# A mixer's order list: the triangular inverse's first step moved up, and five of the delta rule's steps placed between S5's output quarters

## The chip, the cores and the metric

The kernel runs on one core of one Trainium2 chip. A time is the device time of one execution in microseconds (us). The core has five engines that run at once, each with a queue of its own: TensorE (PE in the profile; its weight loads are PEld), VectorE (DVE), ScalarE (ACT), GpSimd (POOL) and SyncE (SP, which issues the transfers here). They wait for each other by semaphores.

## The reference, cut to what matters

```python
for l in range(DEPTH):                       # 2 layers, 272 tokens (16 meta + 256), 1024 features
    h = h + 0.5 * swiglu(rmsnorm(h, ffn1_norm[l]), ...)     # 2816 wide
    h = h + hybrid_mixer(rmsnorm(h, mix_norm[l]), ...)
    h = h + 0.5 * swiglu(rmsnorm(h, ffn2_norm[l]), ...)

def hybrid_mixer(h, w_in, ..., w_out):
    proj = h @ w_in                          # 1024 x 2312
    sb_q, sb_k, sb_v, dn_qkv, dn_z, dn_b, dn_a, s5_u = split(proj)
    o_sb = rmsnorm(stick_breaking_attention(sb_q, sb_k, sb_v))      # 4 heads of 64
    o_dn = gated_deltanet(dn_qkv, dn_z, dn_b, dn_a, ...)            # 4 heads of 64
    o_s5 = rmsnorm(s5_mixer(s5_u, ...))                             # 512 wide, GELU, then a GLU
    return concatenate([o_sb, o_dn, o_s5]) @ w_out

def gated_deltanet(...):
    q, k, v = split(silu(causal_conv4(dn_qkv)))     # q, k L2-normalised per head
    # chunked: T = inverse(I + strict_lower((beta k) k^T * decay)) per chunk,
    # attn = lower(q k^T * decay), then a recursion over the chunks:
    #   v_new = T (beta v - ... k S),  o = q S + attn v_new,  S = S * e^g + k^T v_new
    return rmsnorm(o) * silu(z)
```

## The kernel before

Features lie on the 128 partitions and tokens along the free axis, so the residual stream is eight blocks of 128 x 272 (`xT`). Each product of a weight with the stream is made of three matmuls in a reduced fp32 form: both operands are split into a high and a low part (`wh`, `wl`, `xh`, `xl`; `mm3`, lines 141 to 143). `weights` loads a block of 512 KB, ScalarE copies out the high part (line 133), and VectorE, or for a few blocks by number GpSimd, subtracts for the low part (line 136). The products inside the groups are plain fp32 matmuls.

The change is in `mixer`, which each layer runs once between its two feed-forward parts. Its steps are functions or generators, and the string `MIX` is the order in which they are traced: a letter names a step, a digit its block; a letter without a digit advances a generator to its next `yield`. The program order that follows is a priority: a planner then fixes each engine's queue at compile time, earlier steps first, and puts a later step's instruction ahead where it counts on an earlier one not being ready. On the chip each queue runs in the fixed order. The letters that matter:

- `C0` to `C5`: projections and convolutions of the delta rule's q (0, 1), k (2, 3) and v (4, 5). `U`, `Q`, `K`, `V`, `Z`: projections of S5's input, of the attention's q, k, v, and of the gate z. Each is one block of weights and 24 matmuls (`unit`).
- `g` (`dn_gates`, 7 steps): gates, k's norm, the decay matrix `E`; the last one makes `LT`, k's products times the decay (`dn_products`, line 883).
- `i` (`dn_inverse`, 9 steps): the inverse of the unit lower triangular matrices. The first step gathers the diagonal blocks (`L32`, `LT8`, `r8` on VectorE), spreads them by one matmul (line 995), and solves the 8 x 8 blocks on GpSimd with a row of 14 dependent small operations (lines 1009 and 1010). The others double the block size by small matmuls; the last one (line 1078) completes `TTf`.
- `r` (`dn_rest`, 11 steps): r1 the norms of q (`pn`, line 1099), r2 q's products (`dn_products`, into `E`), r3 the transposes of v and k (line 1114), r4 `pvn`, the first product with `TTf` (line 1153), r5 the first state (`pS`, lines 1159 and 1161), r6 `pk` with that state (line 1143), r7 and r8 the second chunk's `pvn` and `pS`, r9 to r11 the last 16 tokens (`pkt`, `pvt`). r1 to r3 need only the convolutions after their SiLU, not the inverse.
- `l`: SiLU of q and v, then ScalarE's table for GELU. `p`, `t`, `y`: S5's inputs, states and outputs of one quarter (`pY`, lines 845 and 847, with GELU). `x`: the GLU in two halves (`pglu`).
- `a` (`sb`, 10 steps): the attention; the last two (`pob`, line 1275) are its outputs. `v` transposes its values.
- `n`: ScalarE's table for Ln and Exp. `m`: the norm factor `R5` of S5's part. `S4`, `S6`, `S0`, `S2`: the rows of `w_out` that S5's part feeds; their evictions (`sy`, line 1424) need `R5`. `o`: the delta rule's norm and output (`po`). Behind the list come the other rows of `w_out`, four blocks, and the next part's norm.

PSUM has four tags of two buffers each. The tag a step uses:

```python
def s5_outputs(self, u, r):     p = self.psum("b", "pY")
def dn_rest(self, qkv):         psum = lambda nm: self.psum("d", nm)     # r4 to r11
    pn = self.psum("b", "pn")                                            # r1
    self.dn_products(qn, AT, ATt, "b")                                   # r2, three tiles
    pv = self.psum("b", "pv")                                            # r3, three tiles
```

In SBUF the scratch tag `cv` has three buffers, which r1, `Z`, the GLU, the attention's outputs and `sy` share.

Of the kernel before, what the change touches and what calls it, by code (L numbers as in the profile page):

```python
# [38 lines left out]

MIX = "C2 C3 U0 g U1 g g U2 g g g U3 g Q0 p0 p1 Q1 t0 p2 p3 K0 i t1 K1 a a t2 C0 a a i C1 i t3 a a i C4 i a a i C5 l i " \
      "y0 V0 i y1 V1 i y2 Z0 y3 Z1 v r r r r x r r x r n a r r r r a m S4 S6 o S0 S2"
ON_POOL = (5, 7, 10, 15, 20, 25)
NBUF = (3, 2, 3)
LO_POOL = 5
# [14 lines left out]
class Trunk:  # L61
# [1283 lines left out]
    def mixer(self, l, nxt):  # L1345
# [7 lines left out]
        with ExitStack() as es:  # L1353
# [54 lines left out]
            def w_out_part(x, d0, tag):  # L1408
# [11 lines left out]
                for j in range(2):  # L1420
                    x_, p = self.xT[:, d0 + j, t0:], ps[j][:, :T - t0]
                    if x == "S":
# [11 lines left out]
                         m=lambda: self.rms(self.acc, 4 * 512, 0, self.R5, "b"))  # L1434
            for x in MIX.split():
                if x in chains:
# [53 lines left out]
```

## Time and profile before

| | us |
|---|---|
| median of 3 runs (lowest to highest) | 1174.08 (1170.92 to 1177.52) |
| the profiled execution | 1172.99 |
| its span, first to last instruction | 1170.9 |
| TensorE busy in it | 1140.0 (97%) |
| VectorE busy | 858.5 (73%) |
| ScalarE busy | 620.5 (53%) |
| GpSimd busy | 194.0 (17%) |
| mean granted TensorE clock | 0.983 |

Layer 0's mixer lies at about 228 to 390 us of the span, layer 1's at about 808 to 972 us. A window's row gives, for a stretch of the span, each engine's busy time with its number of instructions, the clock granted to TensorE as a share of 2.4 GHz, and the share and rate of the transfers. A timeline's row gives the start, the time, the engine, the line, the operation with the names of its output and inputs, its shape and the number of instructions that were merged; in brackets the engine's idle time just before it and what ended it.

### The profile page before, as it was taken

What the parts mean: (1) busy time and instruction counts of PE and PEld (TensorE: products, weight loads), DVE (VectorE), ACT (ScalarE), POOL (GpSimd) and SP (SyncE); (2) the same over time, 40 slices, a digit from 0 to 9 for tenths busy, and PEclk for the clock granted to TensorE, in tenths of its full rate; (3) what the DMA queues carried; (4) which work ended last, traced back from release to release, by engine and by line L of the source; (5) the groups of instructions that cost most, each with busy time, mean ns of one, the idle gap of its engine ahead of it and who ended that gap; (6) DMA issues with size and microseconds to landing.
All of it is one profiled execution on the core that took longest, in us unless ns stands there. A gap on an engine that the chain in (4) does not pass through costs nothing.

```text
span 1170.9 us, 23748 instructions
## 1 busy us (share of the span) xinstructions
PE 1140.0 (97%) x9544; PEld 1091.7 (93%) x9544; DVE 858.5 (73%) x1609; ACT 620.5 (53%) x993; POOL 194.0 (17%) x242
## 2 busy tenths in 40 slices
PE   8999999999998999999999999999999989999997
PEld 7999999998896999999999999999988969999985
DVE  7999986599656965565569998756995678666544
ACT  6455465464663654444454555645545737545533
POOL 6312101113310111110202111011141001111100
PEclk9999999999998999999999999999999979999998
DMA  5655544542221455555565565455332216556663
GB/s 186 183 174 174 169 149 151 166 127 60 87 73 55 146 172 173 176 180 163 184 180 168 167 193 163 137 179 156 107 91 74 85 43 198 181 181 189 191 196 109
DMA packets 196858, 173.74 MB, mean 148 GB/s; under 512 B 21300, under 2 KB 193004, under 8 KB 196748
## 3 DMA queue, kind: packets, MB, share of 16 engines
q1 hardware_dynamic: 196732, 172.22, 48.6%
q8 instruction: 75, 1.23, 0.4%
q14 instruction: 35, 0.29, 0.1%
q10 hardware_dynamic: 16, 0.00, 0.0%
HBM read 171.15 MB, written 1.05 MB: 147 GB/s over the span
## 4 chain that ended last, share of the span: by engine, by line
PE 83%; DVE 10%; POOL 2%; ACT 2%; issue 2%; DMA 1%; SPq 0%; ACTq 0%; DVEq 0%; POOLq 0%
PE proj L143 17%; PE proj L142 17%; PE proj L141 17%; PE pd L143 5%; PE pd L142 5%; PE pd L141 5%; PE pd L490 5%; DVE wl L136 2%; PE pY L847 1%; POOL TT L1010 1%; PE pm L780 1%; POOL t L1009 1%; PE pob L1275 1%; PE pY L845 1%; DVE s5z L836 1%
## 5 line engine op out<-in xcount | busy, mean ns | idle before, releaser
L141 PE MATMUL proj<-xh,wh 128*128 128x272 f32 (+1 forms) x1840 | 524.8, 291 | 1.5 <-DVE sy L1424 1.5
L142 PE MATMUL proj<-xl,wh 128*128 128x272 f32 (+1 forms) x1840 | 521.9, 290 | 0.3 <-DVE xl L1222 0.3
L143 PE MATMUL proj<-xh,wl 128*128 128x272 f32 (+1 forms) x1840 | 493.4, 291 | 1.5 <-DVE wl L136 1.2
L133 ACT ACTIVATE wh<-raw 128x1024 fp32r<-128x1024 f32 (+1 forms) x324 | 338.2, 1044 | 291.5 <-PE proj L142 102.2
L136 DVE TENSOR_TENSOR wl<-raw,wh 128x1024 fp32r<-128x1024 f32 (+1 forms) x312 | 378.7, 1214 | 146.2 <-PE pd L143 60.5
L141 PEld LDWEIGHTS proj<-xh,wh 128*128 128x128 f32 x1840 | 348.8, 190 | 4.3 <-DVE sy L1424 2.6
L142 PEld LDWEIGHTS proj<-xl,wh 128*128 128x128 f32 x1840 | 348.3, 189 | 2.4 <-DVE xl L1222 0.5
L143 PEld LDWEIGHTS proj<-xh,wl 128*128 128x128 f32 x1840 | 331.4, 189 | 3.9 <-DVE wl L136 2.9
L432 POOL TENSOR_TENSOR hl<-h,hh 128x272 fp32r<-128x272 f32 (+1 forms) x88 | 80.8, 921 | 452.4 <-ACT hh L431 451.5
L141 PE MATMUL pd<-hh,wh 128*128 128x272 f32 x528 | 149.8, 289 | 0.0
L142 PE MATMUL pd<-hl,wh 128*128 128x272 f32 x528 | 149.5, 288 | 0.0
L143 PE MATMUL pd<-hh,wl 128*128 128x272 f32 x528 | 141.1, 289 | 0.2
L141 PEld LDWEIGHTS pd<-hh,wh 128*128 128x128 f32 x528 | 99.3, 188 | 0.2
L142 PEld LDWEIGHTS pd<-hl,wh 128*128 128x128 f32 x528 | 99.4, 188 | 0.1
L143 PEld LDWEIGHTS pd<-hh,wl 128*128 128x128 f32 x528 | 95.2, 189 | 1.0 <-DVE wl L136 0.9
L104 ACT ACTIVATE g<-g 128x272 f32<-128x272 f32 (+2 forms) x92 | 37.7, 415 | 68.8 <-DVE g L426 68.7
L431 ACT ACTIVATE hh<-h 128x272 fp32r<-128x272 f32 (+1 forms) x88 | 36.3, 419 | 50.7 <-DVE h L430 50.6
L430 DVE TENSOR_TENSOR h<-proj,g 128x272 f32<-128x272 f32 (+1 forms) x88 | 37.8, 434 | 32.3 <-PE proj L143 20.6
L426 DVE TENSOR_TENSOR g<-proj,R 128x272 f32<-128x272 f32 (+1 forms) x88 | 37.5, 431 | 18.3 <-PE proj L143 18.1
L428 DVE TENSOR_TENSOR g<-g,R 128x272 f32<-128x272 f32 (+1 forms) x88 | 37.8, 434 | 12.5 <-ACT g L104 12.2
L136 POOL TENSOR_TENSOR wl<-raw,wh 128x1024 fp32r<-128x1024 f32 x12 | 29.4, 2452 | 97.0 <-PE proj L143 31.9
L373 POOL TENSOR_TENSOR acc<-acc,sq 128x272 f32<-128x272 f32 (+1 forms) x20 | 23.1, 1153 | 91.9 <-ACT sq L367 91.3
(490 smaller groups left out, 1295.4 us busy)
## 6 DMA issues: line engine op xcount, KB each, us to landing
raw<-in_ffn_w_gate_dram SPq DMA_DIRECT2D x88, 512.0 KB, 3.6
raw<-in_ffn_w_up_dram SPq DMA_DIRECT2D x88, 512.0 KB, 3.7
raw<-in_ffn_w_down_dram SPq DMA_DIRECT2D x70, 512.0 KB, 3.5
raw<-in_w_in_dram SPq DMA_DIRECT2D x36, 512.0 KB, 4.3
raw<-in_ffn_w_down_dram SPq DMA_DIRECT2D x24, 384.0 KB, 3.0
raw<-in_w_out_dram SPq DMA_DIRECT2D x16, 512.0 KB, 3.4
raw<-in_s_w_glu_dram SPq DMA_DIRECT2D x4, 512.0 KB, 4.7
xin<-in_x_dram SPq DMA_DIRECT2D x4, 256.0 KB, 6.1
```

The lines of the kernel that those rows point to most:

```text
L104: i = self.nc.scalar.activation(out, in_, func, **k)
L133: nc.scalar.activation(h[:, :n], r[:, :n], AF.Copy)
L136: e.tensor_tensor(l[:, :n], r[:, :n], f32(h[:, :n]), op=ALU.subtract)
L141: mm(p, wh, xh, start=first, stop=False)
L142: mm(p, wh, xl, start=False, stop=False)
L143: mm(p, wl, xh, start=False, stop=last)
L426: V.tensor_tensor(g1, pg[j][:, :N], R, op=ALU.mult)
L428: V.tensor_tensor(g1, g1, R, op=ALU.mult)
L430: V.tensor_tensor(h, pu[j][:, :N], g1, op=ALU.mult)
L431: nc.scalar.activation(hh[:, f, :N], h, AF.Copy)
L432: G.tensor_tensor(hl[:, f, :N], h, f32(hh[:, f, :N]), op=ALU.subtract)
L490: PE.matmul(pd[i][e], x[:, f, ts], w[:, 0, e * 512:e * 512 + 512], start=f == 0 and w is h and x is hh, stop=f == NF - 1 and w is lo)
```

## The change

Only the string `MIX` is changed. The inverse's first step `i`, which stood behind `K0`, stands behind the seventh `g`, ahead of `Q0`; the second to the seventh inverse step move up by about one place each, to `K0`, `K1`, `C0`, `C1`, `C4` and ahead of `C5`; the last two stay behind `V0` and `V1`. The first five steps `r`, of which four stood behind `Z1 v` and one behind the GLU's first half, stand behind `l`, `V0`, `y2`, `y3` and `Z1`. The GLU's `x` steps keep their order; r6 stays behind the first, and r7 and r8 stand behind the second, ahead of `n` and the attention's first output.

```diff
--- before.py
+++ after.py
@@ -39,8 +39,8 @@
 
 
 
-MIX = "C2 C3 U0 g U1 g g U2 g g g U3 g Q0 p0 p1 Q1 t0 p2 p3 K0 i t1 K1 a a t2 C0 a a i C1 i t3 a a i C4 i a a i C5 l i " \
-      "y0 V0 i y1 V1 i y2 Z0 y3 Z1 v r r r r x r r x r n a r r r r a m S4 S6 o S0 S2"
+MIX = "C2 C3 U0 g U1 g g U2 g g g U3 g i Q0 p0 p1 Q1 t0 p2 p3 K0 i t1 K1 i a a t2 C0 a i a C1 i t3 a a C4 i a a i C5 l " \
+      "r y0 V0 r i y1 V1 i y2 r Z0 y3 r Z1 r v x r x r r n a r r r a m S4 S6 o S0 S2"
 ON_POOL = (5, 7, 10, 15, 20, 25)
 NBUF = (3, 2, 3)
 LO_POOL = 5
```

## Rows read from the trace of the kernel before

**Rows 1.** Part 1 of the page: busy us, share, instructions.
```profile
PE 1140.0 (97%) x9544; PEld 1091.7 (93%) x9544; DVE 858.5 (73%) x1609; ACT 620.5 (53%) x993; POOL 194.0 (17%) x242
```

**Rows 2.** Windows, layer 0: us, busy us (instructions) per engine, PEclk, DMA.
```profile
224.00:228.00 4.00, 4.00 (x34) 4.00 (x33) 3.53 (x6) 3.06 (x6) 0.50 (x6) 1.00 0.89 247
...
296.00:300.00 4.00, 3.49 (x28) 3.03 (x26) 2.39 (x6) 3.05 (x6) 3.38 (x9) 1.00 0.50 135
300.00:304.00 4.00, 2.13 (x79) 1.68 (x80) 4.00 (x9) 0.81 (x2) 0.11 (x1) 1.00 0.00 0
...
360.00:364.00 4.00, 4.00 (x35) 3.04 (x33) 1.23 (x1) 1.67 (x3) 0.00 (x0) 1.00 0.15 49
364.00:368.00 4.00, 2.02 (x30) 1.49 (x29) 2.52 (x9) 0.98 (x3) 0.00 (x0) 1.00 0.24 82
368.00:372.00 4.00, 3.36 (x24) 1.84 (x25) 2.63 (x7) 1.22 (x3) 0.00 (x0) 0.63 0.01 4
372.00:376.00 4.00, 2.95 (x10) 1.52 (x8) 1.35 (x5) 1.63 (x5) 0.29 (x1) 0.50 0.00 0
376.00:380.00 4.00, 3.57 (x19) 3.25 (x18) 3.96 (x13) 0.95 (x2) 0.00 (x0) 0.59 0.00 0
```

**Rows 3.** The same windows in layer 1's mixer.
```profile
876.00:880.00 4.00, 3.49 (x64) 3.18 (x65) 2.38 (x6) 2.83 (x5) 2.67 (x8) 1.00 0.44 125
880.00:884.00 4.00, 2.58 (x69) 2.13 (x56) 4.00 (x9) 1.34 (x3) 0.11 (x1) 1.00 0.01 4
...
944.00:948.00 4.00, 1.73 (x34) 0.76 (x32) 3.48 (x11) 1.13 (x3) 0.00 (x0) 0.74 0.00 0
948.00:952.00 4.00, 3.93 (x16) 2.06 (x12) 1.67 (x5) 1.02 (x2) 0.00 (x0) 0.50 0.00 0
952.00:956.00 4.00, 2.54 (x8) 1.40 (x8) 2.48 (x8) 1.63 (x5) 0.29 (x1) 0.50 0.00 0
956.00:960.00 4.00, 4.00 (x22) 4.00 (x22) 3.91 (x13) 0.95 (x2) 0.00 (x0) 0.56 0.00 0
```

**Rows 4.** TensorE's timeline at the mixer's end: start, us, line, [idle, releaser].
```profile
361.44 0.67 PE L1275 MATMUL pob<-W 128*64 128x272 f32 x2
...
366.84 0.32 PE L1176 MATMUL pkt<-qkv,kn 64*32 64x64 f32 x7 [1.28 <-DVE qkv L1170]
...
369.26 1.17 PE L1275 MATMUL pob<-W 128*64 128x272 f32 x2 [0.32 <-DVE sby L1284]
...
376.76 0.60 PE L141 MATMUL proj<-xh,wh 128*128 128x272 f32 x1 [0.43 <-DVE sy L1424]
```

**Rows 5.** TensorE's timeline: inverse's end, recursion's steps, the GLU's last product.
```profile
331.55 1.14 PE L1078 MATMUL py<-TTf,X 64*64 64x64 f32 x16
...
340.99 0.50 PE L1099 MATMUL pn<-bd,sq 128*128 128x2 f32 x4
...
347.83 0.29 PE L143 MATMUL pglu<-xh,wl 128*128 128x272 f32 x1
...
351.64 1.11 PE L1153 MATMUL pvn<-vb,TTf 128*128 128x64 f32 x8
...
357.36 0.43 PE L1143 MATMUL pk<-qkv,kn 64*128 64x64 f32 x2
...
363.94 1.10 PE L1161 MATMUL pS<-qkv,E 128*128 128x64 f32 x8
```

**Rows 6.** ScalarE's timeline: the silu step.
```profile
311.26 1.21 ACT L104 ACTIVATE qkv<-qkv 128x544 f32<-128x544 f32 x2
```

**Rows 7.** GpSimd's timeline: the inverse's first step.
```profile
278.95 2.10 POOL L1004 TENSOR_TENSOR Lm<-L,lev 128x288 f32<-128x288 f32 x2 [0.88 <-DVE L L986]
...
299.10 0.80 POOL L1012 TENSOR_TENSOR TT<-TT,m8c 128x288 f32<-128x288 f32 x1
```

**Rows 8.** VectorE: durations of one line (ns, min/median/max); an eviction of r2.
```profile
L825 DVE TENSOR_TENSOR x<-s5z,sn x8: 433/436/1029, 258.2 to 870.6; 128x272 f32<-128x272 f32 x8
...
343.86 0.68 DVE L883 TENSOR_TENSOR E<-pl,E 128x512 f32<-128x512 f32 x1
```

## The prediction

> **What bounds the kernel now.** I read the page's first part, then windows of 4 us through both mixers, then TensorE's timeline in the windows that stood out, and last VectorE's, ScalarE's and GpSimd's timelines for what TensorE waited for there. The page: TensorE is busy for 97% of the span [rows 1]. That leaves 31 us without a matmul, and a busy microsecond need not be a full one. A window of plain projections holds 34 matmuls in 4 us, 0.12 us apart, at a granted clock of 1.00, the 2.4 GHz level; this is the measure [rows 2].
>
> Against it, two places in each mixer fall short. At the end of layer 0's mixer, 364 to 380 us, TensorE is busy 2.02, 3.36, 2.95 and 3.57 us, at clocks of 1.00, 0.63, 0.50 and 0.59 [rows 2]. It loses 4.1 us idle, and of the busy time another 3.36 x 0.37 + 2.95 x 0.50 + 3.57 x 0.41 = 4.2 us to the clock: 8.3 us. The same place of layer 1's, 944 to 960 us, loses 3.8 us idle and 1.73 x 0.26 + 3.93 x 0.50 + 2.54 x 0.50 + 4.00 x 0.44 = 5.4 us to the clock: 9.2 us [rows 3]. Together **17.5 us**; it is an upper bound, since busy times of overlapping matmuls count some of the clock's loss double. The second place, where the attention's scores and the inverse's first matmuls meet, costs 0.51 + 1.87 and 0.51 + 1.42 us idle: **4.3 us** [rows 2, 3].
>
> What is waited for in the tail: the timeline has the delta rule's tokens of the last 16 (`pkt`, 1.28 us idle behind VectorE), then the attention's second output (`pob`), then `w_out`'s products behind `sy` [rows 4]. All of this is chain work with nothing left to lay beside it: the projections are over and the S half of `w_out` has been spent as filler, and what of it remains waits for a PSUM buffer. The slow clock comes with it: the same `pob` product takes 0.67 us for two at the full clock and 1.17 us in the tail [rows 4].
>
> Why the chain is late: the inverse's last product is at 331.55 us, but the recursion's first that uses it, `pvn`, is at 351.64 us [rows 5]. In between stand steps `r`1 to `r`3, which need neither: their first product `pn` is issued at 340.99 us [rows 5], though its operand is ready behind `silu`, which is done at 311.26 + 1.21 = 312.5 us [rows 6]. The list puts them behind `Z1 v`, and the order of the queues keeps to the list while TensorE has earlier work. So a move in the list is a move in the queue.
>
> **The change part by part.** No instruction, transfer or weight block is added or taken away, and the order of the weight blocks among themselves is the same, so SP's queue and the blocks split on GpSimd stay. Everything is order, and the sum is made of idle time and clock, not of durations.
>
> *Steps r1 to r5 go between l and x.* r1 goes right behind `silu`, r2 behind V0, r3 behind y2, r4 behind y3, r5 behind Z1; r6 stays behind the GLU's first half and r7 behind its second; r8 comes in front of the attention's first output instead of behind it. Their own TensorE time is the same on either side. Cover where they go now: V0, V1, Z0 and Z1 are 96 products, 96 x 0.12 = 11.6 us. What it does to the tail, counted from the GLU's last product (347.83 us, call it G) [rows 5]: before, `pvn` (r4) is at G + 3.8, `pk` (r6) at G + 9.5, the last `pS` (r8) ends at G + 17.2. After it, r6 can start 24 products or 2.9 us before G or a little later; r6 to the end of r8 takes 365.0 - 357.4 = 7.7 us in the trace, so r8 ends between G + 4.8 and G + 7.7, and G itself moves back by the products of r4 to r6 put ahead of it, some 4 us by their rows. The chain is then 365.0 - 347.8 - 7.7 - 4 = 5.5 to 8.4 us ahead of where it is now.
>
> Is there enough to lay beside it? Behind G stand the S half of `w_out`, 96 x 0.12 = 11.6 us, two outputs of the attention of 2.1 us each at full clock (two heads; the row gives 0.67 us for a head's first pair), and some 5 us of small products: 21 us. The chain behind r8 is r9 to r11 (365.0 to 369.3 us, 4.2 us) and the delta rule's norm and output, 7.5 us up to the next product of `w_out` (376.76 us); beside it run the two attention outputs, one behind the other, of some 7.5 us each (the first's product at 361.44, the second's at 369.26 us, less its wait of 0.32) [rows 4]. The longer of the two, 15 us, ends at G + 20 to G + 23. So filler and chain are about as long: the tail's loss goes nearly wholly, or 2 us a mixer stay. Bounds: all 17.5 us back, or only what the earlier chain gives in idle time with the clock's part kept, 4 us a mixer, 8 us. I take **13.5 us**, near the upper bound since the window ahead of 364 us is still full at a clock of 1.00 [rows 2], with the chain and the filler side by side, and that is the state the change extends.
>
> *The inverse's first step goes from behind K0 to right behind `g`'s last (k's products).* Its chain is: `LT`, small copies and sums on VectorE, one product, and on GpSimd `Lm` at 278.95 us and a row of small operations up to 299.10 + 0.80 us [rows 7]. Ahead of it on VectorE stood two S5 quarters' states and K's evictions; with these behind it, the chain starts up to 8 us earlier. Queued behind its product on TensorE are Q0 and the quarters' inputs: the product waits in a queue that runs in order, and they with it. In the trace, TensorE's wait for the chain's end (the first product of the next step) and for the scores is the 4.3 us of the second place. Below: these 4.3 us go, since the chain is done before the scores need TensorE. Above: the same wait comes again in front of Q0, 4.3 us more. The nearest rows are the waits themselves, which come from order against real durations and will fall somewhere else rather than go; I take **0.5 us** back.
>
> *The inverse steps i2 to i7* shift by one place (K0, K1, C0, C1, C4, C5); they stand in the same stretch of full TensorE windows, at nothing, hidden by the conv blocks' 24 products each; uncovered they would cost 1 us a step.
>
> Sum: the profiled execution took 1173.0 us, its span 1170.9 and 2.1 around it. 1173.0 - 13.5 - 0.5 = 1159.0. The median of the runs is 1.1 us above the profiled one, so 1160.
>
> **GpSimd beside VectorE.** The row: while `Lm` runs on GpSimd, 2.10 us for two, VectorE's slowest product with `sn` of layer 0 takes 1.03 us; the median of the eight is 0.44 us [rows 7, 8]. Per microsecond of GpSimd that is 0.6 us of VectorE. The Trainium skill (GPSIMD Engine Reference, section 8, Key points) says that GpSimd shares its SBUF interfaces with VectorE and contends with VectorE instructions that have two SBUF inputs; the S5 states are of that kind, and by that rule the moved chain would lengthen them. Where the chain ends now, VectorE is busy 2.39 of 4 us [rows 2]: some 3 us of GpSimd's time find a partner less busy than it would be earlier. At 0.6 that is at most 2 us a mixer, and I take none in the sum, since most of the chain already runs beside the S5 states.
>
> **The rivals.**
> 1. *The wait moves within the tail.* r7, r8, then the attention's outputs stand in nearly the same order as before, with the same two buffers of tag d and three of tag cv; `sy` may still wait for a cv buffer behind the second output, and with it S0 and S2. For it: the row of 376.76 us waits on `sy` [rows 4]. Then only half comes back: 13.5 / 2, 1173 - 7 = 1166 us, with the median 1167.
> 2. *Contention of GpSimd and VectorE* as above, where VectorE sets the pace: 2 x 2 us off the gain, 1164.
> 3. *No change.* TensorE has 97%, its work is the same, and each stall taken away reappears before the mixer's end. Against it: the slow clock is a loss that only sparse stretches have. 1173.
> 4. *Slower: PSUM tag b.* r1 to r3 use seven buffers of tag b (pn, three products, three transposes) between the four quarters' `pY`, two at a time. A tile is held from product to eviction: r2's first product follows `pn`, from 341.5 us, and VectorE is done with it at 343.86 + 0.68 = 344.5 us, 3 us [rows 5, 8]. 7 x 3 / 2 = 10.5 us by which y3, and the GLU behind it, can be late. The cover is 11.6 us of V and Z products. If the planned order has spent them before, TensorE stands idle for up to 10.5 us a mixer; the S half, which needs the GLU, then comes late as filler too, so half of the tail's gain stays away. It decides from 3.5 us a mixer on, where it eats the 7 us left, and at its full price gives 1173 + 21 - 7 = 1187, by the median 1188.
>
> **How the numbers follow.** Chances: the forecast 0.53, rival 1 0.18, rival 2 0.05, rival 3 0.12, rival 4 0.12. A change of 0.5% is 5.9 us, about what a measurement of this kernel can tell from none: faster is below 1168.2, slower above 1180.0. Faster: 0.53, 0.05 and six tenths of rival 1, 0.69, less a little for the forecast's own upper end: 0.68. Slower: rival 4 where it costs over 6.5 us a mixer, 0.10, and 0.01 for the second place's wait doubled in front of Q0 with nothing gained. The rest 0.21. The range: at the low end all of the tail and of the second place come back, 1174.1 - 17.5 - 4.3 = 1152, and 1151 for what the windows leave out; at the high end rival 3's 1173. Outside stay rival 4 and a few hundredths. The forecast's own range is 1152 to 1166, its bounds 17.5 + 4.3 and 8 us.
>
> **What would show it.** In the changed profile `pn` (L1099) stands near 313 us instead of 341, `pvn` (L1153) ahead of the GLU's products, within 5 us of the inverse's last; the tail's windows hold over 3.8 us of TensorE at 1.00, and the granted clock's mean rises above 0.983. `Lm` runs some 5 to 8 us earlier. I am wrong if the tail still shows 0.50, if TensorE's idle time in front of the GLU grows (`pY` late, rival 4), or if the second place's wait turns up before Q0 with more than 4 us.

## The result, and the profile after

The changed kernel takes **1189.7 us** (median of 8 runs, 1179.4 to 1191.1) against 1172.6 us for the kernel before (8 runs): a ratio of 1.0117, 95% interval 1.0079 to 1.0154. It is slower by 1.2%, where 1160 us and a gain of 1.1% were forecast. Ratios here leave out runs over 1.5% above the fastest of the same kernel (five of the ten in the changed kernel's second measurement, one of six each in e15 and e17), and so do the mean clocks below.

Each run comes with the span and the mean of TensorE's granted clock, and for the changed kernel the one goes with the other: 1179.4 us at 0.981, 1180.0 at 0.979 (the profiled one), 1185.7 at 0.975, 1188.6 at 0.972, three at 1190.9 with 0.969 to 0.973, 1191.1 at 0.968. Span times mean clock is 1153.9 us, as a mean of the 8 runs. For the kernel before it is 1154.0 (29 runs beside the first experiments, mean clock 0.984). By this reckoning the work is the same and the loss is clock. It is a first reading only, since a slow clock costs nothing while TensorE waits; it says where to look.

The page's first part, for the changed kernel; TensorE's share is unchanged [rows 1]:

```profile
PE 1147.2 (97%) x9544; PEld 1101.3 (93%) x9544; DVE 857.0 (73%) x1609; ACT 618.5 (52%) x993; POOL 189.9 (16%) x242
```

Windows of 4 us, as in [rows 2]: us, busy us (instructions) of TensorE, its weight loads, VectorE, ScalarE, GpSimd, then the granted clock. First between `silu` and the GLU, then the tail:

```profile
320.00:324.00 4.00, 4.00 (x83) 3.65 (x80) 1.63 (x4) 0.37 (x1) 0.00 (x0) 1.00 0.02 4
324.00:328.00 4.00, 4.00 (x39) 3.92 (x38) 0.43 (x1) 0.37 (x1) 0.00 (x0) 0.78 0.00 0
328.00:332.00 4.00, 4.00 (x27) 3.76 (x27) 0.10 (x1) 1.55 (x4) 0.00 (x0) 0.50 0.00 0
332.00:336.00 4.00, 4.00 (x20) 4.00 (x20) 0.32 (x1) 0.38 (x1) 0.00 (x0) 0.50 0.00 0
336.00:340.00 4.00, 4.00 (x20) 4.00 (x20) 0.87 (x3) 1.89 (x5) 0.00 (x0) 0.51 0.02 4
...
364.00:368.00 4.00, 3.40 (x41) 2.62 (x39) 3.00 (x8) 2.79 (x6) 0.00 (x0) 1.00 0.15 50
368.00:372.00 4.00, 4.00 (x32) 2.80 (x30) 3.40 (x9) 2.31 (x6) 0.00 (x0) 1.00 0.39 133
372.00:376.00 4.00, 2.47 (x17) 1.99 (x16) 2.20 (x5) 2.47 (x7) 0.00 (x0) 1.00 0.00 0
376.00:380.00 4.00, 2.92 (x14) 2.92 (x15) 4.00 (x14) 0.50 (x2) 0.29 (x1) 0.68 0.38 131
```

The tail is better, as forecast: at 368 to 376 us the clock is 1.00 where it was 0.63 and 0.50 [rows 2]. But a new place is slow. From 324 to 340 us TensorE is busy for all of its time and idles nowhere, and for 13.7 of these 16 us it runs at 0.50, its 1.2 GHz level: 4 x (0.22 + 0.50 + 0.50 + 0.49) = 6.8 us. Layer 1's windows from 908 to 924 us give 0.74, 0.50, 0.50 and 0.55, another 6.8 us. In the kernel before this stretch ran at 1.00.

TensorE's timeline of the changed kernel (start, us, line, operation), with the steps of [rows 5]:

```profile
311.71 0.50 PE L1099 MATMUL pn<-bd,sq 128*128 128x2 f32 x4
...
313.89 0.44 PE L845 MATMUL pY<-s5U,M 128*128 128x68 f32 x2
...
318.57 0.39 PE L141 MATMUL proj<-xh,wh 128*128 128x272 f32 x1
...
323.06 0.29 PE L141 MATMUL proj<-xh,wh 128*128 128x272 f32 x1
...
325.65 0.61 PE L847 MATMUL pY<-s5z,W 128*128 128x68 f32 x4
...
326.34 1.06 PE L847 MATMUL pY<-s5z,W 128*128 128x68 f32 x4
...
329.89 1.97 PE L1078 MATMUL py<-TTf,X 64*64 64x64 f32 x16
...
337.68 0.57 PE L142 MATMUL proj<-xl,wh 128*128 128x272 f32 x1
...
342.19 1.10 PE L1153 MATMUL pvn<-vb,TTf 128*128 128x64 f32 x8
...
351.30 0.52 PE L141 MATMUL pglu<-xh,wh 128*128 128x272 f32 x2
...
358.21 0.29 PE L143 MATMUL pglu<-xh,wl 128*128 128x272 f32 x1
...
377.08 0.39 PE L141 MATMUL proj<-xh,wh 128*128 128x272 f32 x1 [2.61 <-DVE sy L1424]
```

`pn` and `pvn` went where the list sends them. The same four products of `pY` (L847) take 0.61 us at 325.65 and 1.06 us from 326.34 us on: here the clock fell. The GLU's last product comes at 358.21 us instead of 347.83 [rows 5].

How many full products (128 x 272) of the projections lie in 26 us behind `pn`'s new place: the window view for `proj` alone (us, TensorE busy, count), first of the kernel before, then of the changed kernel; behind the counts again the granted clock.

```profile
312.00:338.00 26.00, 12.32 (x88) 11.07 (x86) 1.71 (x4) 1.00 0.20 63
```

```profile
312.00:338.00 26.00, 2.86 (x17) 2.49 (x18) 0.35 (x1) 0.77 0.12 41
```

88 full products before, 17 after. S5's outputs and the inverse's products stood between them; now these are packed together with r1 to r3, products of 1 to 128 columns. The counts overstate it: the slow clock itself makes the second one smaller, and `silu` is 3 us earlier in the changed kernel. Over 26 us from the end of its first half (from 311.9 and from 308.9 us) the same view counts 89 and 40. What the order alone gives is the length of the stretches without a full product: at most 3.8 us in the kernel before (y3, 330.39 to 334.21 us); in the changed kernel 6.9 us from `pn` on (311.71 to 318.57 us) and 14.4 us up to the first transposes of r3 (323.3 to 337.68 us, most of it at the slow clock). In the second the clock fell.

A sum over each mixer, from the starts in TensorE's timeline: first product of the gates to the GLU's first; the GLU's first to its last; from there to the next norm's product (`pms`).

| us | layer 0 before | after | layer 1 before | after |
|---|---|---|---|---|
| gates to GLU | 96.9 | 110.6 | 94.5 | 110.6 |
| in the GLU | 10.2 | 6.9 | 10.2 | 8.3 |
| GLU to `pms` | 57.8 | 49.7 | 56.3 | 48.8 |

The change moves 13.7 and 16.1 us ahead of the GLU and gets 11.4 and 9.4 us back: 9.0 us lost. The rest of the span is 1.8 us shorter, and 9.0 - 1.8 = 7.2 us is the difference of the profiled spans (1178.1 and 1170.9). Of the 29.8 us ahead of the GLU, two times 6.8 are clock.

### The profile page after: what moved, and what is told of

It is laid out like the page before. It is cut to its first block, busy times and chain, and to the rows that moved or that the text cites. A ratio compares the mean times of both kernels' runs of the same rounds, so it can differ in the third digit from the quotient of the medians.

```text
span 1178.1 us, 23742 instructions
## 1 busy us (share of the span) xinstructions
PE 1147.2 (97%) x9544; PEld 1101.3 (93%) x9544; DVE 857.0 (73%) x1609; ACT 618.5 (52%) x993; POOL 189.9 (16%) x242
## 4 chain that ended last, share of the span: by engine, by line
PE 82%; DVE 12%; ACT 2%; issue 2%; POOL 1%; DMA 0%; SPq 0%; ACTq 0%; DVEq 0%; POOLq 0%
PE proj L143 17%; PE proj L142 17%; PE proj L141 17%; PE pd L143 5%; PE pd L142 5%; PE pd L141 5%; PE pd L490 5%; DVE wl L136 2%; PE pY L847 2%; PE pY L845 1%; DVE s5U L809 1%; PE pm L780 1%; DVE s5z L829 1%; POOL t L1009 1%; POOL TT L1010 1%
```

## The experiments

Theory 1: the granted clock falls on the packed run of small products, although TensorE is never idle. Theory 2: S5's last outputs and the GLU come late (rival 4's buffers), and the filler behind them with it. Theory 3: the inverse's first step costs.

**The changed kernel again, and its two parts apart.** The first is the changed kernel itself. The second has the inverse's moves alone, the third the recursion's alone, the fourth is the changed kernel with r1 to r3 on PSUM tag c.

```
e1_only_i   ... U3 g i Q0 ... K0 i t1 K1 i a a t2 C0 a i a C1 i t3 a a C4 i a a i C5 l   (rest as before)
e2_only_r   (start as before)   r y0 V0 r i y1 V1 i y2 r Z0 y3 r Z1 r v x r x r r n a r r r a ...
e3_tag_c    - pn = self.psum("b", "pn")        + pn = self.psum("c", "pn")
            - self.dn_products(qn, AT, ATt, "b")  + self.dn_products(qn, AT, ATt, "c")
            (pv and pvt alike)
```

> The changed kernel once more, for a second profile beside the others of the same chip. Every theory: slower than before, 1179 to 1191 us. Theory 1 (the clock): the time goes with the granted clock's mean, and the stretch of S5's outputs between the SiLU and the GLU again has a spell at 0.50 of 13 us or more in each mixer. Theory 2 (the late GLU): the GLU's products start some 10 us later than before whatever the clock does.

> Only the inverse's steps are moved, the recursion's stand where they were. If the loss comes from the recursion's steps (theories 1 and 2), this is the kernel before within 4 us, 1169 to 1176, with no spell at 0.50 between the SiLU and the GLU. If it comes from the inverse's first step in front of Q0 (theory 3), 1180 or more.

> Only the recursion's steps are moved, the inverse's stand where they were. Theories 1 and 2: all of the loss is here, 1179 to 1191, with S5's first output behind the SiLU instead of at 278 us, the outputs in one block with r2 and the inverse's last steps, and a spell at 0.50 there. Theory 3: 1172 or less.

> The changed list, but r1 to r3 take their seven PSUM tiles from tag c, not b, so that S5's outputs need not wait for them. Theories 1 and 2 (the tag is what holds the outputs back): S5's first output is at 278 us again, the GLU starts within 5 us of where it started before, no spell of 13 us, and what the early recursion gives in the tail shows: 1160 to 1172. Theory 3: still 1180 or more. If small products between projections are costly wherever they stand: 1175 to 1185.

Measured: the changed kernel again 1192.7 us (ratio 1.0056, 1.0018 to 1.0095; its 10 runs spread over 1175 to 1207 us). Its profile shows the spell in both mixers, as expected, and longer than in the first profile (windows as above):

```profile
315.90:346.60 30.70, 30.70 (x229) 29.06 (x224) 4.35 (x10) 6.29 (x17) 0.00 (x0) 0.50 0.02 6
906.40:940.50 34.10, 34.10 (x248) 32.34 (x248) 5.78 (x12) 7.51 (x18) 0.22 (x2) 0.50 0.03 11
```

Here the clock fell already in the first stretch without a full product, some 5 us behind `pn`: the moment differs between two executions of one kernel.

The inverse alone 1174.2 (1.0003, 0.9978 to 1.0028): theory 3 falls. The recursion alone 1185.6 (1.0086, 1.0056 to 1.0116): the loss is its. Tag c 1185.2 (1.0085, 1.0057 to 1.0113). With tag c the first `pY` is again at 275 us and not behind `silu`, but y3 and the GLU stay late, the 26 us hold 47 full products, and the clock there is 0.80. So the tag is not what costs, and the 1160 to 1172 us that theories 1 and 2 had expected from it were wrong. The loss is of another make here: span times mean clock is 1159.8 us against 1154.0, so about half of the 11 us is not clock; what that half is was not followed up.

The third kernel holds a comparison in itself. Behind `silu`, whose first half ends at 311.8 us in layer 0 and at 893.9 us in layer 1, its two mixers run nearly the same products in the same order. The window view for `proj`, in each layer the first 17 us from there and the next 9:

```profile
311.80:328.80 17.00, 5.50 (x40) 4.84 (x38) 0.85 (x2) 1.00 0.21 64
328.80:337.80 9.00, 2.56 (x20) 2.58 (x21) 0.44 (x1) 1.00 0.01 2
893.90:910.90 17.00, 5.77 (x42) 5.11 (x40) 0.87 (x2) 1.00 0.22 64
910.90:919.90 9.00, 0.00 (x0) 0.00 (x0) 0.00 (x0) 0.51 0.01 2
```

For 17 us both layers do the same at the full clock. Then, in the stretch of y1, the inverse's last product and y2, which holds no full product (9.2 us long at the full clock, 326.1 to 335.3 us of layer 0), the clock falls in layer 1 and stays up in layer 0. So such a stretch can lower the clock and need not, and the count behind the fall is its consequence.

**A run of small products without any step of the recursion.** The kernel before, with V0, V1 and Z0 drawn out from between the quarters:

```
- l i y0 V0 i y1 V1 i y2 Z0 y3 Z1 v r r ...
+ l i V0 V1 Z0 i y0 y1 i y2 y3 Z1 v r r ...
```

> The list of the kernel before with one thing changed: V0, V1 and Z0 are taken from between the quarters of S5's outputs and stand ahead of them, so that y0 to y3 and the inverse's steps follow each other as a run of about 15 us of small plain fp32 products, with no step of the recursion moved and the GLU behind the same work as before. Theory 1 (a run of small products lowers TensorE's granted clock although TensorE is never idle): a spell at 0.50 of some 7 to 14 us between the SiLU and the GLU in both mixers, the row pY of line 847 near 1.06 us in it instead of 0.61, and a time 7 to 14 us above before, 1180 to 1188. Theory 2 (the loss came from the recursion's steps themselves, by the buffers that they hold or by a GLU that falls behind them): clock near 1.00 between the SiLU and the GLU as in before, time within 0.3% of before, 1171 to 1178.

Measured: 1185.4 us, 1.0097 (1.0076 to 1.0118), mean clock 0.973. Its windows:

```profile
324.00:328.00 4.00, 4.00 (x51) 3.85 (x49) 0.43 (x1) 1.53 (x4) 0.00 (x0) 1.00 0.00 0
328.00:332.00 4.00, 4.00 (x34) 3.76 (x32) 0.00 (x0) 1.55 (x4) 0.00 (x0) 0.67 0.00 0
332.00:336.00 4.00, 4.00 (x19) 4.00 (x19) 0.42 (x1) 1.52 (x4) 1.80 (x1) 0.50 0.02 4
336.00:340.00 4.00, 4.00 (x21) 4.00 (x20) 0.88 (x2) 1.57 (x5) 0.00 (x0) 0.55 0.00 0
```

No product of the recursion is moved, TensorE is busy throughout, and the clock falls all the same, at about the price of the change itself. Theory 1 holds, for this kernel at least: bunching is enough. Whether it is the products' size or their plain fp32 form that counts no run separates, since the full products differ from them in both.

**Full products added to the changed kernel.** These read an operand that is at hand and write a PSUM tile that nobody reads; they only add work.

```
e6   in s5_outputs, behind each of the 4 blocks of every quarter:   + self.spare(3, ...)
e13  + if r in (1, 2) and b % 2: self.spare(12, ...)      e15: 24 in place of 12
e14  + if r == 0: self.spare(12, ...)     e16: 6 in place of 12
e17  + if r == 3: self.spare(6, ...)
def spare(self, n, k, tag, after):
    p = self.psum(tag, "pspare")
    for j in range(n):
        i = self.nc.tensor.matmul(p[:, :T], self.xh[:, k, 16:144], self.xh[:, k, :], start=True, stop=True)
        ...
```

> The changed kernel with work added and nothing moved: behind each of the 16 blocks of S5's outputs three full products (128 x 272, like those of the projections, about 0.12 us each) whose result nobody reads, 48 in each mixer, about 6 us at full clock. Theory 1: the run of small products is broken up, no spell at 0.50 longer than 3.4 us stands between the SiLU and the GLU, and the clock gives back about what the added work takes: 1178 to 1193, against 1186 to 1190 for the changed kernel. Theory 2 (the clock is not what makes the stage long): the added work comes on top, 12 us for both mixers, 1198 to 1204, and the spell stays.

Measured: 1204.8 us, 1.0278 (1.0251 to 1.0305), mean clock 0.972. The time is theory 2's. The profile splits it; whole windows over the stage in layer 0 and in layer 1:

```profile
316.00:340.00 24.00, 24.00 (x288) 22.59 (x288) 5.96 (x14) 7.21 (x19) 1.38 (x4) 1.00 0.08 25
912.00:936.00 24.00, 24.00 (x147) 22.86 (x146) 1.79 (x5) 3.85 (x10) 0.00 (x0) 0.57 0.01 1
```

The order around the two stretches is the same, the clock is kept in one and lost in the other, although no stretch without a full product is longer than 3.3 us at the full clock. Inconclusive, so the products were gathered:

> The changed kernel with 48 full products added in each mixer (6 us at full clock, nobody reads their result) as four blocks of twelve inside the run of small products: behind the second and the fourth block of y1 and of y2. Theory 1 (it is that run that lowers the clock): the mean clock rises from 0.9735 to 0.983 or more, the spell at 0.50 between the SiLU and the GLU is gone or at most 3.4 us long, and the time is 1182 to 1192, about that of the changed kernel, although 12 us of work were added. The rival (the run is not what lowers it): mean clock 0.970 to 0.976, 1200 to 1206.

> The control: the same 48 products as four blocks of twelve, behind the four blocks of y0, ahead of the run instead of in it. Theory 1: the run behind them stays, the spell too, mean clock 0.970 to 0.977, 1198 to 1206. The rival (any added full products in this stage do what the twelve in the run do, or none does): the same clock and time as the kernel with the products in the run, within 0.3%.

> Twice the products inside the run: four blocks of 24 in each mixer, 24 us in all at full clock. Theory 1: no spell at 0.50 between the SiLU and the GLU in either mixer, mean clock 0.985 or more, 1193 to 1203 (span times mean clock near 1179). The rival: mean clock 0.970 to 0.976 and 1212 to 1220.

Measured: e13 1198.7 us (1.0198, 1.0155 to 1.0242; clock 0.976), e15 1215.3 (1.0342, 1.0316 to 1.0369; 0.972), and the control e14 1182.4 (1.0092, 1.0056 to 1.0128; 0.988). That is the reverse of what was expected: the control kept the clock from `silu` to within 0.3 us of the GLU in both mixers of its profiled run, the slowest of the six, and with some 12 us of work added (96 x 0.12) its median is 7 us below the changed kernel's, though the intervals of the two ratios, taken at different times, overlap. TensorE's timeline of e13 says why (its L856 is L847 of the other kernels):

```profile
315.43 0.61 PE L856 MATMUL pY<-s5z,W 128*128 128x68 f32 x4
...
316.11 1.06 PE L856 MATMUL pY<-s5z,W 128*128 128x68 f32 x4
...
335.99 0.80 PE L800 MATMUL pspare<-xh 128*128 128x272 f32 x2
```

The clock had fallen by 316.11 us, the first added products come 20 us later. I had put the run's beginning at y1; it begins with `pn` and y0, as in the second profile of the changed kernel. Products put there break it up, products behind the fall come too late. This reading was then put to a test of its own, half the products at y0 and the same number at y3:

> The changed kernel with 24 full products added in each mixer (3 us at full clock, nobody reads their result), six behind each of the four blocks of y0, where the kernel with twelve in each of these places had its clock at 1.00 from SiLU to GLU. Theory 1, with the run beginning at pn and y0: mean clock 0.982 or more, no spell at 0.50 over 3.4 us between the SiLU and the GLU in at least one mixer, 1174 to 1184, below the changed kernel although work was added. The rival (what kept the clock up there was the planner's other order of the filler): 1188 to 1198 at a mean clock of 0.970 to 0.977.

> The control: the same 24 products, six behind each block of y3, behind the point where the clock has fallen in the changed kernel. Theory 1: the spell before y3 stays in both mixers, mean clock 0.970 to 0.978, 1190 to 1200. The rival: the same as with the products at y0, within 0.3%.

Measured: at y0 1181.0 us (1.0067, 1.0044 to 1.0091; clock 0.987), at y3 1195.9 (1.0161, 1.0118 to 1.0205; 0.975). Both as theory 1 says, and on the same chip the intervals do not touch. The planner's order of the other filler differs between the two as well: the second stretch without a full product, 9.2 us long at the full clock in the third kernel, is 6.9 to 7.3 us in e14 and e16, so the added products are not the only difference. Against the changed kernel itself the gain shows in the medians: over the median of the kernel before, measured beside them, they are 1.0146 and 1.0151 for its two measurements, 1.0076 for e14, 1.0055 for e16. The ratios above do not separate e14 and e16 from the 1.0056 of the second one.

**The recursion moved, but not into S5's outputs.** Without added work: the first r stands right behind y3, two behind Z1.

```
- y2 Z0 y3 Z1 v r r r r x r r x r n a r r r r a m S4 S6 o S0 S2
+ y2 Z0 y3 r Z1 r r v r x r r x r r n a r r r a m S4 S6 o S0 S2             (e7)
+ y2 Z0 y3 r Z1 r r v r x r r x r r m n a r S4 r S6 r S0 S2 a o             (e8)
```

> The list of the kernel before, with only the recursion's steps drawn ahead of where they stand, and none of them ahead of the last quarter of S5's outputs: the first right behind y3, two behind Z1, the others one or two places earlier among the GLU's columns. Theory 1: S5's outputs run as in before at full clock, no spell at 0.50 longer than 3.4 us stands between the SiLU and the GLU's end, and the recursion ends up to 5 us earlier in each mixer than in before; the tail gives 1 to 4 us in each mixer, 1166 to 1173. The rival (moving the recursion's operands ahead of the GLU costs wherever they stand): 1180 to 1188.

> As the kernel with the recursion's steps behind y3, and besides the end of the attention stands last in the list and the products of the S half of the output projection ahead of it, so that 56 full products lie between the second attention block and its norm. Theory 1 with the tail's clock as the second loss (4.3 to 5.6 us in each mixer in before): the granted clock between the recursion's second state and the output projection is above 0.9 instead of near 0.6, 1162 to 1170. The rival (the products in the tail have to wait for their own operands, so that the chain behind them is held back by the same time): no gain, 1172 to 1182.

Measured: e7 1173.7 us, 1.0001 (0.9982 to 1.0020), mean clock 0.988; 75 full products in 312 to 338 us at 1.00. So moving the recursion ahead is not what costs, but neither does it gain: from the GLU's last product to `pms` the mixers are 5.0 and 4.6 us shorter than before, from the gates to that product 3.0 and 6.0 us longer. e8 1186.8 us, 1.0113 (1.0089 to 1.0138): the chain came late, its first `po` 388.3 - 350.0 = 38.3 us behind the GLU's last product, against 375.46 - 347.83 = 27.6 us before. Its rival held, and cost more than it had been given. Its profile shows where: TensorE waits 2.29 us for VectorE's `nt` in front of r8, the clock is at 0.50 from 364.3 us on, and the 56 products then run between the second `pob`, done at 379.2 us, and its norm (`pnb`) and `po`.

**The tail's clock.** The kernel before, its list unchanged, with added full products behind the steps of the tail's chain, 30 in each mixer (e9) or 15 (e10); 30 with the inverse's moves (e11) or with e7's list (e12).

```
  i = PE.matmul(pn[:, :T], self.bd64, r, start=True, stop=True)
+ if b == 0: self.sp = self.psum("c", "pspare")
+ self.spare((10, 4)[b], i)
  ...
+ (pkt) self.spare(6, i)   (pvt) self.spare(3, i)   (second pob) self.spare(4, i)   (first po) self.spare(3, i)
```

> The kernel before, its list unchanged, with work added in the tail alone: full products (128 x 272) whose result nobody reads behind the steps of the chain there, 10 behind the first pnb, 6 behind pkt, 3 behind pvt, 4 behind the second pob, 4 behind the second pnb, 3 behind the first po; 30 in each mixer, 3.7 us at full clock, in a stretch in which TensorE idles 4.3 to 4.9 us in all. Theory 1 (the granted clock of 0.50 in the tail is the greater part of what the tail loses, and it falls because TensorE has little to do there): clock near 1.00 in 364 to 384 us of the first mixer, 4 us less in each mixer for the clock and up to 1.5 us more for products that come in the chain's way, 1164 to 1170. The rival (the chain's own latencies set the tail and the clock only fills them): the time is that of before or more, 1173 to 1181.

> As the kernel with 30 added products in the tail, with 15 in their place (5, 3, 2, 2, 2 and 1), 1.9 us in each mixer. Theory 1: if half of them keep the clock up, the time is 1162 to 1169; if they are too few, the spell at 0.50 in the tail stays and the time is 1172 to 1178. The rival: 1173 to 1177.

> The kernel with only the inverse's steps moved, and the 30 added products in its tail. Its span times its mean granted clock was 1151.5 us against 1154.0 to 1154.5 of before, so if theory 1 holds for the tail and the added products give back 8 us of the clock, this is below the kernel before with the same products by 1 to 3 us: 1161 to 1168. The rival (the move of the inverse's first step gives nothing of its own): the time of the kernel before with the same products, within 0.2%.

> The kernel with the recursion's steps behind y3 (span times mean clock 1158.1 us, 13.6 us below full clock), and the 30 added products in its tail, where the clock spell is 3.4 us long in each mixer. Theory 1: little is left to give back, 1.7 us in each mixer, and the products take about as much: 1170 to 1176. The rival for the tail (the chain's latencies): 1174 to 1182.

Measured: e9 **1170.3 us, 0.9959 (0.9944 to 0.9974)**, clock 0.995; e10 1169.9, 0.9970 (0.9953 to 0.9987), 0.994; e11 1170.2, 0.9967 (0.9952 to 0.9983), 0.994; e12 1171.8, 0.9989 (0.9968 to 1.0010), 0.994. The first three beat both kernels, by 0.3 to 0.4%: less than expected (1161 to 1170). e11 equals e9, so the inverse's move gives nothing of its own. The tail in e9:

```profile
364.00:368.00 4.00, 3.89 (x49) 2.78 (x50) 2.70 (x9) 1.32 (x3) 0.00 (x0) 1.00 0.02 4
368.00:372.00 4.00, 2.63 (x17) 2.01 (x16) 2.01 (x8) 1.45 (x5) 0.00 (x0) 1.00 0.00 0
372.00:376.00 4.00, 4.00 (x32) 3.81 (x32) 3.96 (x13) 1.08 (x3) 0.44 (x1) 1.00 0.00 0
376.00:380.00 4.00, 4.00 (x34) 4.00 (x33) 3.96 (x11) 1.70 (x2) 0.53 (x1) 1.00 0.05 6
```

The clock is 1.00 throughout, and yet the stretch from the GLU's last product to `pms` is 57.6 and 55.3 us, against 57.8 and 56.3 before. Of the 4 to 5 us that I had counted as the clock's in each tail only 0.2 and 1.0 come back, with 30 x 0.12 = 3.6 us of products added; a part of these fills idle time, which falls from 4.9 to 2.8 and from 4.3 to 2.5 us. The runs do not separate what the clock gave from what the added products took. A part of the gain is lost again to waits for VectorE. The second `pnb` ends 25.0 us behind the GLU's last product instead of 27.1, but then TensorE waits:

```profile
371.81 0.39 PE L141 MATMUL proj<-xh,wh 128*128 128x272 f32 x1 [1.37 <-DVE sy L1439]
```

(L1439 is L1424 of the kernel before.) The other 3 us of e9's gain lie outside the tails, where nothing was edited; where they come from the runs don't settle.

## Why the prediction was wrong

**The step that failed** is the cost of r1 to r5: "Their own TensorE time is the same on either side. Cover where they go now: V0, V1, Z0 and Z1 are 96 products, 96 x 0.12 = 11.6 us." (96 x 0.12 is 11.5.) The products were counted as cover for waits, and the clock at the new place was put at nothing. Nothing waits there: TensorE has no idle time to speak of between `silu` and the GLU. What the projections did between S5's outputs was to keep full products coming. With the steps drawn in front of them, and y0 drawn behind `silu`, stretches of 6.9 us and more without one are left, and the same work ran at 0.77 of full clock. A run of the bunch alone, without r, costs about the same (e5), the same r behind y3 costs nothing (e7), and full products at the head of the run pay for themselves by the medians (e14, e16). In the profiled run this is 2 x 6.8 us; the median is 10 us above the profiled run, at a lower clock.

The premise that fits it is said in the prediction's third rival: "the slow clock is a loss that only sparse stretches have". The trace of the kernel before had already shown otherwise, in a third place of layer 0's mixer that the prediction passes over, where the gates' and S5's products meet:

```profile
260.00:264.00 4.00, 4.00 (x16) 2.90 (x16) 4.00 (x10) 0.77 (x2) 0.11 (x1) 0.50 0.20 57
```

TensorE is busy for all of the 4 us, at 0.50. With the windows beside it (0.98 and 0.67) the spell is 6.8 us long.

The Trainium skill (TensorE: Matmul & The Clock Gate, Part 1: The HAM clock gate) describes a gate that is set by how busy TensorE has been, and its first example of a loss is a TensorE that waits for DMA. This trace differs: windows of 4.00 busy us in 4, with no wait, ran at 0.50. The Trainium skill also says there that the point at which the clock rises at a kernel's start varies from run to run. For the fall the runs here show the same and more: e6 lost its clock in one mixer and kept it in the other, and the changed kernel's mean clock lies between 0.968 and 0.981.

**The tail's 13.5 us** did not come back in full. The chain is earlier, as forecast (r8's products end at 358.81 + 1.10 = 359.9 us, 1.7 us behind the GLU's last, against 17.2 before), and the clock at 368 to 376 us is 1.00. From the GLU's last product to `pms`, layer 0 and layer 1, first of the kernel before, then of the changed kernel:

```profile
347.83:405.61 57.78, 52.85 (x406) 46.54 (x406) 45.97 (x99) 28.74 (x53) 5.44 (x5) 0.91 0.28 90
926.86:983.19 56.33, 52.04 (x409) 45.63 (x409) 44.87 (x99) 28.41 (x53) 5.19 (x5) 0.88 0.31 99
```

```profile
358.21:407.87 49.66, 45.80 (x351) 41.51 (x350) 43.02 (x90) 29.30 (x53) 5.18 (x5) 0.97 0.37 117
942.40:991.17 48.77, 43.98 (x353) 39.58 (x352) 42.39 (x90) 29.27 (x53) 5.61 (x5) 0.97 0.42 130
```

The clock rose, from 0.91 and 0.88 to 0.97. The idle time, of which the sum had 4.1 and 3.8 us in the tail's windows and took most as gained, stayed: 4.9 and 4.3 us before, 3.9 and 4.8 after. The stretch is shorter by 8.1 and 7.5 us mostly because work moved out of it, and that work comes back ahead of G, the GLU's last product: from the gates, G is 10.4 and 14.3 us later, 6.8 of each by the new slow clock; the remaining 3.6 and 7.5 us stand against the "some 4 us" of r4 to r6, in which r3 and the product of r7, ahead of G now too, were left out. Without the 13.6 us of clock the table above would give 9.0 - 13.6, a gain of 4.6 us at best where 14.0 were forecast, and e7, which keeps the clock, gives none. Nor is it shown that the tail's slow clock adds to its idle time as a loss: e9 kept the tail at 1.00, and it was only 0.2 and 1.0 us shorter.

**The inverse's first step**, 0.5 us: not contradicted, and too small to be measured (1.0003, 0.9978 to 1.0028). `Lm` starts 2.6 us earlier (276.37 us), not 5 to 8. The idle time of the second place went from 4.3 to 2.1 us in both layers together.

**The rivals.** Rival 4 named the right steps and buffers: y0 loses the tag b buffers that it had ahead of `silu`, y3 ends at 347.8 us instead of 334.4 and the GLU's last product is 10.4 us late. But TensorE stood idle nowhere; it ran slow, and with tag c the loss was the same within the intervals. That its 1188 us is near the 1189.7 measured is luck. Rival 1 is half there: `sy` now holds TensorE up for 2.61 us instead of 0.43 [rows 4], more than half of the idle time that the tail keeps. Rival 2's contention wasn't tried by itself; with 1.0003 (to 1.0028) for the inverse's moves there is little room for its 4 us. Rival 3, no change, is what e7 does.

## What to carry over

Before moving work, look at what stands between the small products, not only at who waits for whom: a stretch with TensorE busy for all of its time can lose half its clock when full products are drawn out of it. Look for windows at 0.50 with TensorE fully busy in the trace before the change, too. Compare span times mean granted clock of the two kernels first; if it is the same, look for the loss in the clock, at the windows at 0.50 that are new. A slow clock beside a chain that waits on other engines may be no reserve: price it by filling the gap, not by the clock's row. And count what is moved out of a place as time at the place where it goes.

## What was not expected of the hardware

TensorE falls to its 1.2 GHz level while it is never idle: plain fp32 products of 1 to 128 columns, busy 4.00 of 4.00 us, clock 0.50. The same order of products keeps the clock in one mixer and loses it in the other (e6, the third kernel); what decides it stays open. And added work can save time: e9 does some 7 us more (60 x 0.12) than the kernel before and takes 0.4% less.
